# A two-layer decoder trunk on one core: turned attention product, and the seven-product form of the first half's first MLP from its first rows on

## The chip, the core and the metric

The kernel runs on one core of a Trainium2 chip. The metric is the device time of one execution in microseconds (us). Before the change it is 2275.01 us in the median of three runs (2270.06 to 2276.08).

## The reference, cut to what matters

The input is 1024 rows of width 1024 in float32, and two layers follow each other. Layer 0 mixes by sliding-window attention and, beside it, a gated DeltaNet of four heads; layer 1 mixes by a gated linear recurrence. After each mixer stands a layer norm, then an MLP with squared ReLU, then another layer norm.

```python
o = jnp.einsum('bnhgqk,bnkhd->bnqhgd', p.astype(v.dtype), vb)   # attention: softmax weights times values
...
def sqrelu_mlp(x, w1, w2):
    h = jax.nn.relu(x @ w1)
    return (h * h) @ w2
...
for layer in range(DEPTH):
    ...
    x = layer_norm(DN_ALPHA * x + mix, ln1_g[layer], ln1_b[layer])
    x = layer_norm(DN_ALPHA * x + sqrelu_mlp(x, mlp_w1[layer], mlp_w2[layer]), ln2_g[layer], ln2_b[layer])
```

There are 8 query heads of width 64 on 2 key heads, and a block of 128 rows sees its own 128 keys and those of the block before. The hidden width of the MLP is 4096.

## The kernel before, in words

**Two streams.** The rows are cut into two halves of 512, each a Python generator (`stream`): stream 0 for the first half, stream 1 for the second. Each goes through the layer-0 mixer (`hybrid`), its output projection and layer norm (`mix_out`), the first MLP (`mlp_ln`, `mlp`), the recurrence and its projection, and the second MLP. A planner at the end of `trunk` takes pieces from the streams and from a list of side jobs (`mixers`: attention blocks, DeltaNet heads, layer norms, the sums below) by a model of the engines' time, and so writes one fixed order for TensorE (PE); the order on the other engines follows from it. Nothing is reordered at run time.

**Large products.** A product in float32 is split into three in a rounded format (`mm3`, L206 holds every matmul): high times high, high times low, low times high, each with 128x128 weights and 512 columns moving, summed in a PSUM bank. Weights come by DMA into `ws` (three buffers, issued from the SP queue), are rounded into `wh` and the rest into `wl`, on ScalarE (ACT) or VectorE (DVE). The tiles `wh`, `wl` have three buffers too. PSUM has eight banks: four named `mm` for the large products, four named `mx` for the side jobs.

**The MLP.** It goes over four quarters `j` of the hidden width. In the straight form (`straight`) an eighth of the hidden rows is made with `w1` and at once multiplied with `w2`; a quarter takes 192 products with `w1` and 192 with `w2`. In the seven-product form (`first`, then `seven`) a quarter's hidden rows stay in two granules `g` of SBUF, and the product with `w2` is done as a 2x2 block product with seven block multiplications instead of eight, 168 products, with combinations of the hidden blocks on DVE (1024 elements wide) and four sums of `w2` blocks, `t1` to `t4`, that side job `w2_sums` makes in DRAM beforehand: a copy DRAM to DRAM from the SP queue and an adding copy from the POOL queue for each, 32 pairs in all, paced at 8 us a transfer in layer 0. In `seven` two results stay in PSUM over several block products: X in two `mm` banks, R in two `mx` banks, whose value is needed again with the third and fifth products. `weave` sets two pieces of `seven` beside one of `first` for the next quarter.

Which form is taken is decided at the loop `while e < 8`: the straight form goes on until stream 1 has its output projection in this layer, two granules are free and a quarter ends. Of the first half's first MLP the first two quarters are straight.

**Attention.** `attn_block` scores a block, exponentiates on ACT with the row sums in `den`, scales the weights by 1/`den` in 8 ACT instructions, turns them by transposes on PE (`csb` holds the identity), and multiplies: `vraw` (values, 64 wide) as weights, turned scores of 512 columns moving, plain float32, once for each key block and key head. The result is already turned for the output projection.

**Parked results.** In stream 1 ten projections for the DeltaNet (`park`, source `hin_fm`) are written to DRAM (`parked<-r`) and read back (`f<-parked`) when their head is due. `head_z` and `head_front` then work on them on ACT and DVE; tiles `f` have four buffers. `head_mid` of a head inverts a triangular matrix by steps of 32x32 matmuls (`mx<-t` 32x32), each with a few small DVE instructions between.

Of the kernel before, what the change touches and what calls it, by code (L numbers as in the profile page):

```python
# [17 lines left out]
P = 128  # L18
# [195 lines left out]
def trunk(ctx: ExitStack, tc, I, out):  # L214
# [316 lines left out]
    def mlp(layer, c, yT, yg, ls, res, tail=False):  # L531
# [65 lines left out]
        def seven(j, g, done):  # L597
# [8 lines left out]
            yield from wait(lambda: (layer, j) in summed)  # L606
            A = {f"a{r + 1}{q + 1}": v4(g[q])[:, :, r * 256:(r + 1) * 256] for q in range(2) for r in range(2)}
            bank = {}
            for i, (a, b, acc, out, sign, last) in enumerate((
# [4 lines left out]
                if i == 2:  # L614
                    V.tensor_tensor(A["a21"], A["a21"], A["a22"], ALU.subtract)
                elif i == 3:
                    V.tensor_tensor(A["a21"], A["a21"], A["a11"], ALU.subtract)
                elif i == 4:
                    V.tensor_tensor(A["a12"], A["a12"], A["a21"], ALU.add)
                elif i == 5:  # L620
                    V.scalar_tensor_tensor(A["a21"], A["a21"], -1.0, A["a22"], ALU.mult, ALU.subtract)
                start = i < 3
                if start:
                    bank[acc] = [(mm_ps if acc == "X" else mx_ps)() for _ in range(2)]
                    kept[0] += 2 * (acc == "X")
                for p in range(2):
                    yield from wait(lambda: either(2))
                    ring = either(2)
                    ah, al = ts(ring, F32R), ts(ring, F32R)
                    ah2, al2 = (z.rearrange("p (k t) -> p k t", k=2) for z in (ah, al))  # L630
                    x = A[a][:, 2 * p:2 * p + 2]
                    S.copy(ah2, x)
                    V.tensor_tensor(al2, x, ah2, ALU.subtract)
                    wh, wl = wblock(w2_quarter(layer, j, b)[p * P:(p + 1) * P])
                    for k in range(2):
                        for t in range(2):
                            mm3(bank[acc][t], ah2[:, k, t * P:(t + 1) * P], al2[:, k, t * P:(t + 1) * P], wh[k], wl[k],
                                start and p + k == 0, p + k == 2, not start)
                            if p + k == 2:
                                accumulate(bank[acc][t], 2 * out[0] + t, out[1], sign, done and last)  # L640
                            if k + t < 2:
                                yield
                    free(ring, ah, al)
                    if i == 6 and p == 1:
                        free("g", *g)
                        kept[0] -= 2
                    if done and i in (4, 6) and p == 1:
                        res["n"] = 2 + (i == 6) * 2
                    yield UNIT
# [67 lines left out]

        hids = {}
        e = 0
        while e < 8 and not ((c == 1 or sts[1].get("op", -1) >= layer) and rings["g"] >= 2 and e % 2 == 0):  # L720
            if e == 7:
                res["start"]()
            yield from straight(e, e == 7)
            e += 1
# [93 lines left out]
    def attn_block(c, n, st, oT, tl, o):  # L818
# [34 lines left out]
        S.activation(es, es, AF.Exp)  # L853
        V.tensor_tensor(den, den, es, ALU.add)
        V.reciprocal(den, den)
        for m in (0, 2, 1, 3):
            for g2 in range(2):
                i = 2 * (2 * (m // 2) + g2) + m % 2
                S.activation(pm[m][:, g2, :w], pm[m][:, g2, :w], AF.Copy, scale=den[:, i:i + 1])
        yield at(*pm)  # L860
        po = mx_ps()
        pend = None
        for i, (_, vv) in enumerate(keys):
            for h in range(2):
                ps = mx_ps()
                for g in range(4):
                    PE.transpose(ps[:, g * P:(g + 1) * P], pm[2 * (g // 2) + h][:, g % 2, i * P:(i + 1) * P], ident)
                pT = tl[(6, 7, 2, 3)[2 * i + h]]
                (S.copy if h else V.tensor_copy)(pT, ps)
                yield at(pT)  # L870
                PE.matmul(po[h * 64:(h + 1) * 64, :], vv[:, h * 64:(h + 1) * 64], pT, start=(i == 0),
                          stop=(i == len(keys) - 1))
        h, l = oT.quad(0, n)
        split_ps(h, l, v4(po))
        yield lambda: 0.0


# [501 lines left out]
    def stream(c):  # L1379
        s = dict(ln0=st[c])  # L1380
        xT, oT = xTs[c], ActT()
        yield from hybrid(c, xT, oT, st[c], ("t", "s") if c == 0 else ("t",))
        yield from mix_out(I["hout"], oT, lambda n: I["x"][c * CH + n * P:c * CH + (n + 1) * P, :], 0,
                           "s" if c == 0 else "t", s, st[c]["t"], lambda: c == 0 or "m7" in sts[0])
        phase[c] = 1
        if c == 0:
            spawn(w2_sums())
        yield from mlp_ln(0, c, s, "ts"[c], False)
        phase[c] = 0
        hT = ActT()  # L1390
# [163 lines left out]
```

## Time and profile before

| | |
|---|---|
| median of three runs | 2275.01 us |
| the profiled execution itself | 2275.25 us, of it 2273.5 us from the first to the last instruction |
| PE busy | 2212.7 us (97%) |
| DVE busy | 1546.0 us (68%) |
| ACT busy | 1048.4 us (46%) |
| mean granted TensorE clock | 0.993 |

In the profile, PEld are weight loads on TensorE, POOL is GpSimd, SP the queue that issues most transfers. A row of a group gives what was computed from what, its shape, its count, the busy time in us and the mean of one in ns, then the idle time ahead of it and what ended that. Shares of the clock of 1.00 are full speed. Almost every instruction of ACT and DVE carries L178 and every matmul L206, since helpers issue them; the tile names tell them apart. A plain float32 matmul shows as two instructions.

### The profile page before, as it was taken

How to read it: one execution, taken by the hardware profiler on the slowest of the kernel's cores; microseconds unless marked ns; L12 is line 12 of the kernel's file. 1: busy time of each engine (PE TensorE's matmuls, PEld its weight loads, DVE VectorE, ACT ScalarE, POOL GpSimd, SP SyncE). 2: the span in 40 equal slices, each digit the busy share in tenths (PEclk: the TensorE clock that was granted, in tenths of full speed). 3: DMA queues.
4: the chain of work that ended last, by engine and by line, in shares of the span. 5: the costliest groups of instructions: out<-in, count | busy, mean ns of one | idle time of the engine just before them, and what ended most of it. 6: DMA issues, size and time to landing. Idle time of an engine off the chain costs nothing.

```text
span 2273.5 us, 31954 instructions
## 1 busy us (share of the span) xinstructions
PE 2212.7 (97%) x12436; PEld 1788.5 (79%) x12436; DVE 1546.0 (68%) x2809; ACT 1048.4 (46%) x1878; POOL 28.6 (1%) x56
## 2 busy tenths in 40 slices
PE   8999999989999999999999999999999999999997
PEld 7776877758778887888887878878788887888886
DVE  6787676576555567596567898685566657776477
ACT  5365456244322344454444677373434444444442
POOL 0000000000000000000000000000000000000000
PEclk9999999989999999999999999999999999999999
DMA  4121223256667766677765333323533443444341
GB/s 162 57 77 49 94 79 112 84 181 181 188 199 221 210 209 201 205 251 224 237 214 184 126 134 115 127 83 98 179 103 123 140 145 128 150 169 146 122 164 67
DMA packets 89945, 337.46 MB, mean 148 GB/s; under 512 B 9921, under 2 KB 10305, under 8 KB 81601
## 3 DMA queue, kind: packets, MB, share of 16 engines
q1 hardware_dynamic: 76688, 280.56, 36.2%
q0 software_dynamic: 4608, 33.56, 7.8%
q10 hardware_dynamic: 8496, 21.30, 2.7%
q8 instruction: 97, 1.59, 0.3%
q14 instruction: 56, 0.45, 0.1%
HBM read 324.37 MB, written 78.12 MB: 177 GB/s over the span
## 4 chain that ended last, share of the span: by engine, by line
PE 85%; DVE 7%; ACT 5%; DMA 2%; issue 1%; ACTq 0%; SPq 0%; DVEq 0%
PE mm L206 67%; PE mx L206 17%; DVE g L178 2%; PE mx L210 2%; DVE wl L178 2%; ACT g L178 1%; DVE s L178 1%; ACT s L178 1%; ACT wh L178 1%; DVE t L178 1%; DVE f L178 1%; ACT t L178 1%; ACT f L178 1%; DMA f<-parked 1%; DMA parked<-r 0%
## 5 line engine op out<-in xcount | busy, mean ns | idle before, releaser
L206 PE MATMUL mm<-g,wh 128*128 128x512 f32 x2816 | 885.6, 396 | 1.1 <-DVE g L178 1.1
L178 DVE TENSOR_TENSOR wl<-ws,wh 128x1024 fp32r<-128x1024 f32 (+1 forms) x444 | 538.3, 1212 | 398.9 <-ACT wh L178 394.4
L178 ACT CAST wh<-ws 128x1024 fp32r<-128x1024 f32 (+1 forms) x356 | 371.3, 1043 | 663.4 <-PE mm L206 551.3
L206 PEld LDWEIGHTS mm<-g,wh 128*128 128x128 f32 x2816 | 521.5, 189 | 109.1 <-DVE g L178 2.8
L206 PE MATMUL mm<-g,wl 128*128 128x512 f32 x1408 | 550.3, 391 | 0.0
L206 PE MATMUL mm<-wh,s 128*128 128x512 f32 x1152 | 377.4, 394 | 0.7 <-DVE g L178 0.7
L206 PEld LDWEIGHTS mm<-g,wl 128*128 128x128 f32 x1408 | 265.4, 188 | 56.5
L206 PEld LDWEIGHTS mm<-wh,s 128*128 128x128 f32 x1152 | 216.9, 188 | 46.5 <-ACT s L178 1.1
L206 PE MATMUL mm<-wh,g 128*128 128x512 f32 (+1 forms) x768 | 240.0, 384 | 7.1 <-ACT wh L178 6.8
L206 PE MATMUL mm<-wl,s 128*128 128x512 f32 x576 | 224.8, 390 | 0.0
L206 PE MATMUL mx<-wh,s 128*128 128x512 f32 x576 | 187.9, 392 | 1.5 <-DVE s L178 1.5
L206 PEld LDWEIGHTS mm<-wh,g 128*128 128x128 f32 x768 | 143.3, 191 | 34.1 <-ACT wh L178 6.8
L178 ACT CAST s<-g 128x512 fp32r<-128x512 f32 x172 | 104.7, 622 | 103.2 <-PE mm L206 54.2
L178 DVE TENSOR_TENSOR s<-g,s 128x512 fp32r<-128x512 f32 x172 | 116.0, 685 | 44.3 <-ACT s L178 44.2
L206 PE MATMUL mm<-wl,g 128*128 128x512 f32 (+1 forms) x384 | 144.2, 375 | 0.2 <-DVE wl L178 0.2
L206 PEld LDWEIGHTS mx<-wh,s 128*128 128x128 f32 x576 | 108.2, 188 | 24.6 <-DVE s L178 2.4
L206 PEld LDWEIGHTS mm<-wl,s 128*128 128x128 f32 x576 | 108.6, 189 | 21.4 <-issue 0.2
L206 PE MATMUL mx<-wl,s 128*128 128x512 f32 x288 | 112.1, 389 | 0.0
L178 DVE CAST wh<-ws 128x1024 fp32r<-128x1024 f32 x88 | 60.4, 687 | 65.0 <-PE mm L206 57.7
L178 DVE TENSOR_TENSOR g<-g,mm 128x512 f32<-128x512 f32 x136 | 89.0, 682 | 11.9 <-PE mm L206 11.3
L178 ACT ACTIVATE g<-mm 128x512 f32<-128x512 f32 x100 | 59.2, 592 | 75.2 <-PE mm L206 75.2
L206 PEld LDWEIGHTS mm<-wl,g 128*128 128x128 f32 x384 | 73.5, 192 | 11.6 <-DVE wl L178 0.5
(234 smaller groups left out, 2390.7 us busy)
## 6 DMA issues: line engine op xcount, KB each, us to landing
ws<-w SPq DMA_DIRECT2D x232, 512.0 KB, 3.4
ws<-t SPq DMA_DIRECT2D x96, 512.0 KB, 3.4
t<-w POOLq DMA_DIRECT2D x32, 1024.0 KB, 9.1
ws<-hin_fm SPq DMA_DIRECT2D x32, 512.0 KB, 3.3
t<-w SPq DMA_DIRECT2D x16, 1024.0 KB, 6.8
t<-t SPq DMA_DIRECT2D x16, 1024.0 KB, 6.3
ws<-rin SPq DMA_DIRECT2D x32, 512.0 KB, 3.3
ws<-hout SPq DMA_DIRECT2D x16, 512.0 KB, 3.7
```

The source lines that it names most:

```text
L178: r = f(*a, **k)
L206: ins = self.pe.matmul(out, lhsT, rhs, start=start, stop=stop, skip_group_check=fresh)
L210: return self._pe(self.pe.transpose(out, x, ident), out, [x], 0.00042 * 2 * out.shape[-1])
```

## The change

It has four parts.

1. Attention: the exponentials are no longer scaled on ACT. The turned scores serve as weights (128x128) and the values move (64 columns), 16 matmuls a block (8 in the first), into one bank `po`, one after the other. One DVE instruction multiplies `po` by 1/`den` into `y`, four transposes on PE turn `y`, and the split into high and low part follows as before.
2. `seven` gets a form `brief` while stream 1 has not had its output projection in this layer: the third product is added to two outputs at once, and the fifth begins a fresh pair of `mx` banks, so R is held for one product only.
3. The choice of the form: the MLP of the first half in layer 0 waits for four free granules and then starts with `seven` at once; in layer 1 the straight form ends ahead of stream 1's projection only if all 14 granules are free.
4. `w2_sums` is spawned ahead of the first half's first output projection instead of behind it.

```diff
+            brief = sts[1].get("op", -1) < layer
...
-                    ("a21", "t1", "R", (1, 1), 1, False), ("a21", "t2", "X", (0, 1), -1, False),
+                    ("a21", "t1", "R", ((1, 1), (0, 1)) if brief else ((1, 1),), 1, False),
...
-                start = i < 3
+                start = i < 3 or brief and i == 4
...
-                                accumulate(bank[acc][t], 2 * out[0] + t, out[1], sign, done and last)
+                                for out in outs:
+                                    accumulate(bank[acc][t], 2 * out[0] + t, out[1], sign, done and last)
...
-        while e < 8 and not ((c == 1 or sts[1].get("op", -1) >= layer) and rings["g"] >= 2 and e % 2 == 0):
+        room = lambda: rings["g"] >= (2 if c == 1 or sts[1].get("op", -1) >= layer else
+                                      4 if layer == 0 else GB)
+        yield from wait(lambda: c == 1 or layer == 1 or room())
+        while e < 8 and not (room() and e % 2 == 0):
...
-        for m in (0, 2, 1, 3):
-            for g2 in range(2):
-                i = 2 * (2 * (m // 2) + g2) + m % 2
-                S.activation(pm[m][:, g2, :w], pm[m][:, g2, :w], AF.Copy, scale=den[:, i:i + 1])
...
-                PE.matmul(po[h * 64:(h + 1) * 64, :], vv[:, h * 64:(h + 1) * 64], pT, start=(i == 0),
-                          stop=(i == len(keys) - 1))
+                yield lambda: 0.0
+        yield at(*pT.values())
+        po = mx_ps()
+        for g in range(4):
+            for h in range(2):
+                o = po[:, (2 * g + h) * 64:(2 * g + h + 1) * 64]
+                for i, (_, vv) in enumerate(keys):
+                    PE.matmul(o, pT[i, h][:, g * P:(g + 1) * P], vv[:, h * 64:(h + 1) * 64], start=(i == 0),
+                              stop=(i == len(keys) - 1))
+        y = tl[3]
+        V.tensor_tensor(y.rearrange("p (i d) -> p i d", i=8), po.rearrange("p (i d) -> p i d", i=8), bc_last(den, 64),
+                        ALU.mult)
+        yield at(y)
+        ps = mx_ps()
+        for g in range(4):
+            PE.transpose(ps[:, g * P:(g + 1) * P], y[:, g * P:(g + 1) * P], ident)
...
+        if c == 0:
+            spawn(w2_sums())
         yield from mix_out(I["hout"], oT, lambda n: I["x"][c * CH + n * P:c * CH + (n + 1) * P, :], 0,
...
-        if c == 0:
-            spawn(w2_sums())
```

Over the whole program, the orders of before and after differ in these counts on PE: products of 512 columns 48 fewer (two quarters in the seven-product form, 24 fewer each); 30 matmuls `64x512` of attention gone, 120 of `128x64` in their place (60 and 240 instructions); 32 more transposes. On DVE 44 instructions more, on ACT 44 fewer.

The order on PE around the first half's first layer norm, before. `mm` rows with `wh_5187` are the first products of its first MLP, `csb` rows from `g_4290` and `g_4291` the transposes of the normed rows, `mx<-t` 32x32 the inversion in a head of the second half.

```order
L206 MATMUL mm_5024<-g_2008,wl_5021 128x512
L206 MATMUL mx_5077<-t_4413 32x32 x16
L210 MATMUL mx_5096<-csb,g_4290 128x128 x4
L210 MATMUL mx_5124<-csb,g_4291 128x128 x4
L210 MATMUL mx_5134<-csb,g_4291 128x128 x4
L206 MATMUL mx_5144<-t_4413 32x32 x16
L210 MATMUL mx_5162<-csb,g_4291 128x128 x4
L210 MATMUL mx_5169<-csb,g_4291 128x128 x4
L206 MATMUL mm_5191<-g_4818,wh_5187 128x512
L206 MATMUL mm_5191<-g_4819,wh_5187 128x512
```

The same place after, where `g_4160` and `g_4161` are the normed rows and `mm_4926` is a parked projection of the second half:

```order
L206 MATMUL mm_4926<-g_2041,wl_4923 128x512
L210 MATMUL mx_4942<-csb,g_4160 128x128 x4
L210 MATMUL mx_4952<-csb,g_4160 128x128 x4
L206 MATMUL mm_4926<-g_2041,wh_4922 128x512
L206 MATMUL mm_4926<-g_2042,wh_4922 128x512
L206 MATMUL mm_4926<-g_2041,wl_4923 128x512
L210 MATMUL mx_4962<-csb,g_4160 128x128 x4
L210 MATMUL mx_4990<-csb,g_4161 128x128 x4
L206 MATMUL mm_4926<-g_2041,wh_4922 128x512
L206 MATMUL mm_4926<-g_2042,wh_4922 128x512
L206 MATMUL mm_4926<-g_2041,wl_4923 128x512
```

Before, 96 products of parked projections stand between the output projection and the first product of the MLP, and five of the eight groups of transposes stand behind the last of them. After, 168 stand there: 72 that stood ahead of the output projection (216 there before, 144 now) have moved behind it. They lie among the transposes, and 60 large products stand between the last of the transposes and the MLP.

The order on PE inside an attention block, before, `mm_4628` being a projection that lies beside it:

```order
L206 MATMUL mm_4628<-wh_4671,g_1136 128x512
L206 MATMUL mx_4687<-g_147,vraw_3099 64x512
L210 MATMUL mx_4704<-csb,g_146 128x128 x2
L210 MATMUL mx_4704<-csb,g_147 128x128 x2
L206 MATMUL mm_4629<-wh_4671,g_1135 128x512
L206 MATMUL mm_4629<-wl_4672,g_1135 128x512
L206 MATMUL mm_4629<-wh_4671,g_1136 128x512
L206 MATMUL mm_4626<-wh_4715,g_1371 128x512
```

And after, from the last transposes of a block (`mx_3972`) to its first products with the values:

```order
L210 MATMUL mx_3972<-csb,g_146 128x128 x2
L210 MATMUL mx_3972<-csb,g_147 128x128 x2
L206 MATMUL mx_3978<-t_3404 32x32 x16
L206 MATMUL mm_3925<-g_2039,wh_3921 128x512
L206 MATMUL mm_3925<-g_2040,wh_3921 128x512
L206 MATMUL mm_3925<-g_2039,wl_3922 128x512
L206 MATMUL mm_3925<-g_2041,wh_3921 128x512
L206 MATMUL mm_3925<-g_2042,wh_3921 128x512
L206 MATMUL mm_3925<-g_2041,wl_3922 128x512
L206 MATMUL mx_4003<-vraw_3045,g_147 128x64
L206 MATMUL mx_4003<-vraw_3050,g_147 128x64
L206 MATMUL mx_4003<-vraw_3045,g_146 128x64
```

The four groups of transposes that took turns with the matmuls now stand together, and the 16 products of 64 columns follow in one run.

The order on DVE where the parked results are read back, before. `f_5071` is the last gate read back; `f_5642`, `f_5653`, `f_5664` are the reads of the last head; `t_4413` is the inversion of the head before it.

```order
L178 SCALAR_TENSOR_TENSOR f_5070<-f_5070,f_5071 128x512
L178 TENSOR_TENSOR t_4413<-t_4413,mx_5195 128x128
L178 STREAM_TRANSPOSE t_4413<-t_4413 128x128
L178 TENSOR_TENSOR g_4833<-f_5070,g_4832 128x512
L178 SCALAR_TENSOR_TENSOR f_5643<-f_5642,sm,f_5643 128x512 x3
L178 TENSOR_TENSOR t_4413<-mx_5224,csb 128x128
L178 SCALAR_TENSOR_TENSOR f_5654<-f_5653,sm,f_5654 128x512 x3
L178 TENSOR_TENSOR t_4413<-t_4413,mx_5251 128x128
L178 CAST wh_5420<-ws_5418 128x1024
L178 STREAM_TRANSPOSE t_4413<-t_4413 128x128
L178 SCALAR_TENSOR_TENSOR f_5665<-f_5664,sm,f_5665 128x512
```

And after, with `f_5242` as the last gate, `f_5733` and `f_5744` as reads of the last head and `t_4652` as the inversion:

```order
L178 SCALAR_TENSOR_TENSOR f_5241<-f_5241,f_5242 128x512
L178 CAST wh_5493<-ws_5491 128x1024
L178 TENSOR_TENSOR wl_5494<-ws_5491,wh_5493 128x1024
L178 TENSOR_TENSOR g_4812<-f_5241,g_4811 128x512
L178 TENSOR_TENSOR t_4652<-t_4652,mx_5349 128x128
L178 STREAM_TRANSPOSE t_4652<-t_4652 128x128
L178 SCALAR_TENSOR_TENSOR f_5734<-f_5733,sm,f_5734 128x512 x2
L178 TENSOR_TENSOR t_4652<-mx_5377,csb 128x128
L178 SCALAR_TENSOR_TENSOR f_5734<-f_5733,sm,f_5734 128x512
L178 SCALAR_TENSOR_TENSOR f_5745<-f_5744,sm,f_5745 128x512
L178 TENSOR_TENSOR t_4652<-t_4652,mx_5404 128x128
```

In both, small steps of the inversion stand behind instructions that need what was read back; after the change there are two weight instructions (`wh_5493`, `wl_5494`) among them, and the steps lie closer.

More of the change, by code (lines that the diff above doesn't have):

```diff
@@ L608, in seven @@
             bank = {}
-            for i, (a, b, acc, out, sign, last) in enumerate((
[4 rows of a table removed]
+            brief = sts[1].get("op", -1) < layer
+            for i, (a, b, acc, outs, sign, last) in enumerate((
+                    ("a12", "b21", "R", ((0, 0),), 1, False), ("a11", "b11", "X", ((0, 0),), 1, True),
+                    ("a21", "t1", "R", ((1, 1), (0, 1)) if brief else ((1, 1),), 1, False),
+                    ("a21", "t2", "X", ((0, 1),), -1, False),
+                    ("a12", "b22", "R", ((0, 1),), 1, True), ("a21", "t3", "X", ((1, 1),), -1, True),
+                    ("a22", "t4", "X", ((1, 0),), 1, True))):
                 if i == 2:
@@ L855, in attn_block @@
         V.reciprocal(den, den)
-        for m in (0, 2, 1, 3):
-            for g2 in range(2):
-                i = 2 * (2 * (m // 2) + g2) + m % 2
-                S.activation(pm[m][:, g2, :w], pm[m][:, g2, :w], AF.Copy, scale=den[:, i:i + 1])
[L860 to L864, printed above, removed]
+        pT = {}
+        for h in range(2):
+            yield at(pm[h], pm[2 + h])
+            for i in range(len(keys)):
                 ps = mx_ps()
@@ L867, in attn_block @@
                     PE.transpose(ps[:, g * P:(g + 1) * P], pm[2 * (g // 2) + h][:, g % 2, i * P:(i + 1) * P], ident)
-                pT = tl[(6, 7, 2, 3)[2 * i + h]]
-                (S.copy if h else V.tensor_copy)(pT, ps)
-                yield at(pT)
-                PE.matmul(po[h * 64:(h + 1) * 64, :], vv[:, h * 64:(h + 1) * 64], pT, start=(i == 0),
-                          stop=(i == len(keys) - 1))
+                pT[i, h] = tl[(6, 7, 2, 4)[2 * h + i]]
+                (S.copy if i else V.tensor_copy)(pT[i, h], ps)
+                yield lambda: 0.0
+        yield at(*pT.values())
+        po = mx_ps()
+        for g in range(4):
+            for h in range(2):
+                o = po[:, (2 * g + h) * 64:(2 * g + h + 1) * 64]
[9 more added lines that the diff above has]
+            PE.transpose(ps[:, g * P:(g + 1) * P], y[:, g * P:(g + 1) * P], ident)
         h, l = oT.quad(0, n)
-        split_ps(h, l, v4(po))
+        split_ps(h, l, v4(ps))
         yield lambda: 0.0
```

3 rows, old and new, of the table bank are left out of this document.

## The prediction

> **What bounds the kernel now.** I read the page first, then the table of windows in pieces of 100 us, then the waits, the chain and the timeline where the windows showed a gap.
>
> The first row of the page: busy time of each engine, its share of the span, its instructions.
>
> ```profile
> PE 2212.7 (97%) x12436; PEld 1788.5 (79%) x12436; DVE 1546.0 (68%) x2809; ACT 1048.4 (46%) x1878; POOL 28.6 (1%) x56
> ```
>
> PE is busy in all but 61 us of 2273.5. So two kinds of gain exist: fewer columns on PE, and those idle 61 us. The windows around the places that the change touches (span of the window, then busy us of PE, PEld, DVE, ACT, POOL, granted clock, busy share of the DMA engines, GB/s):
>
> ```profile
> 400.00:500.00 100.00, 88.73 (x652) 65.92 (x651) 70.79 (x168) 39.72 (x77) 1.04 (x2) 0.95 0.40 129
> 500.00:600.00 100.00, 100.00 (x770) 78.63 (x769) 54.18 (x122) 37.65 (x82) 4.20 (x6) 0.96 0.63 175
> 600.00:700.00 100.00, 100.00 (x762) 80.83 (x761) 55.59 (x127) 38.20 (x91) 4.45 (x6) 1.00 0.70 201
> 1000.00:1100.00 100.00, 100.00 (x443) 82.84 (x442) 68.96 (x88) 47.56 (x64) 2.46 (x3) 1.00 0.75 228
> ...
> 470.00:480.00 10.00, 5.49 (x54) 4.04 (x54) 9.86 (x18) 5.44 (x10) 0.00 (x0) 0.69 0.97 360
> 469.60:508.50 38.90, 27.63 (x312) 19.77 (x302) 25.02 (x45) 14.30 (x26) 1.04 (x2) 0.78 0.65 209
> ```
>
> From 500 us on PE is full while the two straight quarters run; at 1000 us it is full with the seven-product form. The gap of 400 to 500 us lies whole between 469.6 and 508.5: PE is idle there for 38.90 - 27.63 = 11.3 us, at a mean clock of 0.78. What PE waited for between 460 and 510 us (total, times, longest), and the chain there (start, length):
>
> ```profile
> PE mx L206 <- DVE t L178: 8.2, 5, 4.7
> PE mx L210 <- DVE g L178: 3.1, 1, 3.1
> ```
>
> ```profile
> 439.87 8.17 PE mm L206 x36
> ...
> 449.63 2.17 DMA parked<-r
> 451.81 3.06 DMA f<-parked
> ...
> 470.67 7.59 DMA parked<-r
> 478.34 3.77 DMA f<-parked
> 487.25 7.31 DMA f<-parked
> 498.88 4.14 PE mm L206 x9
> 503.82 4.14 PE mm L206 x9
> 508.48 2.27 PE mm L206 x9
> ```
>
> Two things come together. The transposes of the layer norm (the 3.1 us on DVE `g`) have no large products left to lie among: the parked projections are used up and the MLP needs the norm. And ACT and DVE stand still for the last parked results, with steps of a head's inversion queued behind them, for which PE waits in order:
>
> ```profile
> 494.67 0.72 ACT L178 ACTIVATE f<-f,sm 128x512 f32<-128x512 f32 x1 [7.26 <-DMA f<-parked]
> 495.43 0.75 DVE L178 SCALAR_TENSOR_TENSOR f<-f,sm,f 128x512 f32<-128x512 f32 x1 [4.78 <-ACT f L178]
> ```
>
> After the longest wait nine products take 4.14 us, twice, and then 2.27: 3.7 us more, and some 0.4 on the small matmuls among them. That place costs 11.3 + 4.1 = 15.4 us.
>
> **The sevens.** A full stretch gives the price of a large product:
>
> ```profile
> 709.58 96.02 PE mm L206 x423
> ```
>
> That is 0.227 us each. Two quarters lose 24 products each: 48 x 0.227 = **10.9 us off PE**, in a stretch where PE is full, so it comes off the end. What it adds lies beside PE:
>
> ```profile
> L178 DVE TENSOR_TENSOR wl<-ws,wh 128x1024 fp32r<-128x1024 f32 x436 | 532.6, 1222 | 398.5 <-ACT wh L178 394.4
> L178 DVE TENSOR_TENSOR s<-g,s 128x512 fp32r<-128x512 f32 x172 | 116.0, 685 | 44.3 <-ACT s L178 44.2
> L178 DVE TENSOR_TENSOR g<-g,g 128x1024 f32<-128x1024 f32 x24 | 29.3, 1219 | 0.0
> ```
>
> For a quarter, 14 weight blocks instead of 8 and 14 hidden pieces instead of 8 and four combinations: 6 x 1.22 + 6 x 0.685 + 4 x 1.22 = 16.3 us of DVE. The accumulations are 16 either way, since the brief form adds its third product twice. A quarter takes (192 + 168) x 0.227 = 82 us, so DVE goes from 55% to some 75%, near the 69% at which PE was full at 1000 us. I cost it at nothing; without that cover it would be at most 2 x 16 us. Holding R for one product only leaves the four `mx` banks to the side jobs in between, so the heads of the second half do not wait for a seven to end. The wait for four free granules stops only stream 0; the order shows stream 1's parked projections filling the time.
>
> **Attention.** Rows of the old form: a large product, the product with the values (two instructions), four transposes, a large product. Then a single load of 128 weights and four of them in a row (whose matmuls move only 16 columns); then four instructions with 128 columns moving, and the lengths of all such (shortest, median, longest, in ns).
>
> ```profile
> 424.78 0.40 PE L206 MATMUL mm<-wh,g 128*128 128x512 f32 x1
> 425.11 1.07 PE L206 MATMUL mx<-g,vraw 128*64 128x512 f32 x2
> 426.11 0.66 PE L210 MATMUL mx<-csb,g 128*128 128x128 f32 x4
> 426.52 0.48 PE L206 MATMUL mm<-wh,g 128*128 128x512 f32 x1
> ```
>
> ```profile
> 122.91 0.19 PEld L206 LDWEIGHTS mm<-g,wl 128*128 128x128 f32 x1
> ...
> 273.13 0.52 PEld L206 LDWEIGHTS mx<-dsc,csb 128*128 128x128 f32 x4 [0.52 <-DVE dsc L178]
> ```
>
> ```profile
> 123.37 0.60 PE L206 MATMUL mx<-S,t 128*128 128x128 f32 x4
> ```
>
> ```profile
> L206 PE MATMUL mx<-S,t x88: 270/275/377, 114.7 to 694.5; 128*128 128x128 f32 x88
> ```
>
> ```profile
> L206 PE MATMUL mx<-g,vraw 128*64 128x512 f32 x60 | 32.2, 618 | 0.0
> ```
>
> The large product would have made room at 424.78 + 0.227 = 425.01; the next thing began at 426.11. So an old product with values costs 1.10 us, 30 of them 33.0. The new form has 240 instructions, each with a load of 128 weights and 64 columns. It is not in the trace. One load after another in the row of four takes (0.52 - 0.19)/3 = 0.11 us. The stream of 512 columns took 1.07 - 0.62 = 0.45 (618 ns is one of the two, 1.07 both), so 64 columns an eighth of it, 0.056. Lower bound 0.056 each (loads free), upper 0.11 + 0.056 = 0.166 (nothing overlaps). I take 0.11, from the row with the same weights and still fewer columns: 26.4 us, and 8 x 0.2 for entering and leaving. Four more transposes a block at 426.52 - 426.11 = 0.41 are 3.3. Together 31.3 against 33.0: **1.7 us off**, between 14.7 off and 11.7 on.
>
> Here the Trainium skill speaks against the change: its page "TensorE: Matmul & The Clock Gate", Part 3, under what overlaps and what doesn't, says that a weight load overlaps a running matmul only when the row group differs. By that rule all 240 loads would stand in the open and attention would cost 11.7 us more instead. The row of four with 128 columns, all in one row group, does not bear it out here: the four together take 0.60 us, a single one 0.275, so they follow at 0.11, where load and stream one after the other would need 0.22.
>
> The scalings that leave ACT (8 a block) and the DVE instruction that comes (8 x some 0.69, as every one of 512 elements) are off PE's path, but they shorten a block by the time between the sums and the transposes:
>
> ```profile
> 417.76 3.31 ACT L178 ACTIVATE g<-g,asc 128x256 f32<-128x256 f32 x8 [0.18 <-DVE asc L178]
> ```
>
> 3.3 us a block that PE does not wait for, yet the first half's mixer is through earlier: that is why the planner sets its output projection ahead of 72 more parked products. New waits are the matmuls with values for the last copy, and the last transposes for the DVE instruction. Behind the first PE has two triples and an inversion step, 1.8 us, against a copy of 0.7; I cost it at nothing, at most 8 x 0.5.
>
> **The gap at 470 us.** 72 products x 0.227 = 16.3 us of cover move behind the output projection, where the norm's transposes now lie among them. The 3.1 us on the norm go. The parked results stay: the last of them is copied when PE leaves the last parked product. In the quick round above the write was issued 1.6 us after that (448.04 to 449.63), write and read took 5.2, and from a read's landing (482.11) to the end of its DVE work
>
> ```profile
> 484.24 0.69 DVE L178 TENSOR_TENSOR g<-f,g 128x512 fp32r<-128x512 f32 x1
> ```
>
> ```profile
> 469.22 0.45 PE L206 MATMUL mx<-t 32*32 32x32 f32 x32
> ```
>
> are 2.8 (to 484.93): 9.6 us in all. The last row is an inversion step on PE. In the slow round, 7.59 and 3.77 for write and read, it is 15.8. In the new order PE has 36 large products and three inversion steps of some 0.4 until it needs DVE behind that, 9.4 us. The wait is 0.2 to 6.4 us, I take the middle, 3.3. The last head's third read (7.31 above, 4.78 of wait on DVE) now has a weight instruction (1.22) and an inversion step or two more ahead of it on DVE, some 1.7 us, so up to 3.1 remains; 1.7. That leaves 5.0 of the 15.4, **10.4 us off**; the ends are 0.2 and, with another half-clock stretch of 4.1, 13.6.
>
> **The sums** go past the loads for the first output projection on SP. The mean DMA share there is 0.40 (400 to 500 us), and three `ws` buffers are cover, so I cost it at nothing; without them a load behind a sum is late by no more than the 7.31 us above; on POOL nothing is queued behind them that PE needs.
>
> **The sum.** Against the profiled execution's own 2275.25 us (span 2273.5 and 1.75 around it; the median is 0.24 lower): 2275.25 - 10.9 - 1.7 - 10.4 = **2252**. Its own range is 2243 to 2261, by the ends of the gap.
>
> **Rivals.** *The gap stays* (16%): the parked round trips now run beside the sums, which begin earlier, and the whole 15.4 us comes back elsewhere. For it: the one read beside a sum took 7.31 us. Against it: four transfers of 512 KB that shared the 0.97 window have gone from that place. Time 2275.25 - 12.6 = 2263.
>
> *The loads show* (9%): 240 x 0.056 = 13.4 us more, 2266. For it: no row has this shape. Against it: the row of four loads and the row of four matmuls. The rule of the Trainium skill quoted there would give the same.
>
> *Weights come late* (7%), the slower side: a round of `weave` is 24 + 24 products, 10.9 us, and needs three blocks of 512 KB, one in 3.6 us, where the straight form needed one in 5.4. The sums of layer 0 run beside it. The DMA share would lie between the 0.75 of 1000 us, where the sums go more slowly, and half more than the 0.63 to 0.70, all of it. At 0.97 a transfer of 256 KB took 7.59 us; a block would then take some 15, and the buffers cover 10.9 less 2.3 for rounding, 8.6. Each round would be 6.6 us late, and seven of the 14 rounds 46: 2298. It turns the sign from the fifth late round on. Against it: at 1000 us the same form ran full at 0.75 beside sums.
>
> *Nothing gained* (7%): the gap stays and the loads show, 2275.
>
> **How the numbers follow.** About 0.3% of this kernel, 6.8 us, can be told from no change. The forecast has 61%. Faster: 61 + 16 + 9 = 86%; same 7%; slower 7%. The range of 2241 to 2267 takes in the forecast, the first two rivals and some of the cheaper loads; outside are the last two, and some 6% below.
>
> **What would show it.** Right: 240 rows of `mx<-vraw,g` at about 26 us of PE; PE without the 3.1 us wait on `g` and with at most some 5 us on `t` before the MLP; PE full, at clock 1.00, through the first two quarters; 48 large products fewer. Wrong: waits on `wh` or `wl` in those quarters, matmul instructions 0.17 us apart in the attention, or a clock under 0.9 at the start of the MLP.

## The result, and the profile after

The changed kernel takes **2282.26 us** (median of nine, 2277.92 to 2285.74) where the kernel before takes 2270.95: a ratio of 1.0055 [1.0045, 1.0065], 0.55% slower. The prediction was 2252, with 2241 to 2267 as its range. One of the nine runs of before, at 2574 us, is left out of the ratio; the others lie between 2267.16 and 2276.08, with a median of 2270.5.

A caution for the reading: the profiled execution of after is the lowest of its nine (2277.92), and that of before, 2275.25, is one of its higher ones. The two pages differ by less than the kernels do, so a second trace of before, at 2266.31 us, stands beside them below.

The first row of the page after: busy time of each engine, share of the span (2276.1), instructions.

```profile
PE 2202.8 (97%) x12600; PEld 1806.5 (79%) x12600; DVE 1580.9 (69%) x2853; ACT 1039.4 (46%) x1834; POOL 29.4 (1%) x56
```

PE is busy 9.9 us less than before, and yet the span is 2.6 us longer: PE's idle time went from 60.8 to 73.3 us. The saving was made, and came back as waits. The windows of after (span, busy us of PE, PEld, DVE, ACT, POOL, granted clock, DMA share, GB/s) show where:

```profile
340.00:360.00 20.00, 15.21 (x222) 12.72 (x220) 10.42 (x26) 8.05 (x24) 0.82 (x1) 0.91 0.64 167
460.00:510.00 50.00, 39.13 (x436) 30.03 (x435) 27.46 (x53) 16.89 (x31) 1.66 (x2) 0.93 0.65 193
500.00:600.00 100.00, 95.56 (x772) 75.02 (x772) 65.61 (x136) 43.94 (x95) 4.31 (x7) 0.98 0.70 200
600.00:700.00 100.00, 96.70 (x741) 76.88 (x740) 66.87 (x135) 43.23 (x92) 4.07 (x5) 0.98 0.70 206
```

The same two early windows in the second trace of before:

```profile
340.00:360.00 20.00, 19.28 (x140) 15.36 (x139) 12.83 (x40) 11.93 (x36) 0.00 (x0) 1.00 0.54 179
460.00:510.00 50.00, 42.64 (x449) 31.95 (x436) 38.13 (x68) 24.99 (x43) 1.85 (x3) 0.93 0.68 213
```

So PE loses time in three places. At 340 to 360 us PE now loses 4.8 us instead of 0.7. At 460 to 510 it loses 10.9; the profiled execution of the prediction had 11.3 there, but the second trace only 50 - 42.64 = 7.4. And the two new quarters, where PE was full, lose 4.4 and 3.3 us, with the clock below 1.00. What PE waits for in after, in three stretches (300 to 400 us, 460 to 510, 500 to 700; total, times, longest):

```profile
PE mx L210 <- DVE g L178: 5.6, 2, 4.5
...
PE mx L206 <- DVE t L178: 10.9, 4, 6.2
...
PE mx L206 <- DVE t L178: 4.8, 4, 3.0
PE mx L210 <- DVE t L178: 2.8, 1, 2.8
```

PE has no wait on `wh` or `wl` among these, and the weight loads (PEld) wait 0.4 us for each of the two between 500 and 700 us, so the weights of the new quarters come in time. PE waits for `t` and `g`, steps of the heads of the second half that lie on DVE. The same view of before's second trace at 460 to 510:

```profile
PE mx L206 <- DVE t L178: 4.3, 4, 1.7
PE mx L210 <- DVE g L178: 3.0, 1, 3.0
```

The norm's wait on `g` is gone in after, as was forecast; the wait on `t` is more than double that of this trace (and 10.9 for the 8.2 of the profiled execution). Some lines of the chain of after name what is behind it:

```profile
343.50 9.50 DMA parked<-r
353.05 2.67 DMA f<-parked
...
475.69 6.78 DMA parked<-r
482.86 8.69 DMA parked<-r
491.56 2.86 DMA f<-parked
499.73 3.93 PE mm L206 x9
504.05 2.27 PE mm L206 x9
```

These are parked round trips, writes of 256 KB among them, and behind the last of them nine products that take 3.93 us where the next nine take 2.27. The first piece of a DRAM sum on SP's queue, in after and then in the profiled execution of before:

```profile
313.46 0.61 SPq L178 DMA_DIRECT2D t<-w  x1
```

```profile
479.32 0.60 SPq L178 DMA_DIRECT2D t<-w  x1
```

The sums now start 166 us earlier and lie beside every parked round trip. The median of a parked write in 300 to 510 us (last column, us to landing) rose from before to after:

```profile
parked<-r SPq DMA_DIRECT2D x10, 256.0 KB, 2.0
```

```profile
parked<-r SPq DMA_DIRECT2D x10, 256.0 KB, 4.8
```

In the new quarters the cause is another one. The DVE queue of after around the wait that PE has at 671 us (start, length, operation), and PE's own rows there:

```profile
667.40 1.22 DVE L178 TENSOR_TENSOR g<-g 128x1024 f32<-128x1024 f32 x1
668.54 1.22 DVE L178 TENSOR_TENSOR wl<-ws,wh 128x1024 fp32r<-128x1024 f32 x1
669.67 1.22 DVE L178 TENSOR_TENSOR g<-g,g 128x1024 f32<-128x1024 f32 x1
670.81 0.68 DVE L178 TENSOR_TENSOR g<-g,mx 128x512 f32<-128x512 f32 x1
671.41 0.28 DVE L178 TENSOR_TENSOR t<-t,mx 128x128 f32<-128x128 f32 x1
671.60 0.68 DVE L178 TENSOR_TENSOR g<-g,mx 128x512 f32<-128x512 f32 x1
672.20 0.68 DVE L178 TENSOR_TENSOR s<-g,s 128x512 fp32r<-128x512 f32 x1
672.80 1.22 DVE L178 TENSOR_TENSOR wl<-ws,wh 128x1024 fp32r<-128x1024 f32 x1
673.94 0.30 DVE L178 STREAM_TRANSPOSE t<-t 128x128 f32<-128x128 f32 x1
```

```profile
671.04 0.39 PE L206 MATMUL mm<-g,wl 128*128 128x512 f32 x1
674.39 0.65 PE L206 MATMUL mx<-t 32*32 32x32 f32 x32 [2.96 <-DVE t L178]
674.97 1.22 PE L206 MATMUL mm<-g,wh 128*128 128x512 f32 x2
```

DVE works without a break from 667.40 to 674.24. Two of its pieces, `g<-g` and `g<-g,g` of 1024 elements, are combinations of the seven products. Behind them, the stream transpose that an inversion's next matmuls need is done only at 674.24; PE, which takes its work in order, stands 2.96 us for it, and the two products behind take 1.22 us where a pair took 0.62 or 0.63 just before.

### The profile page after: what moved, and what is told of

It reads as the page before. It is cut to its first block, busy times and chain, and to the rows that moved or that the text cites. A ratio compares the mean times of both kernels' runs of the same rounds, so it can differ in the third digit from the quotient of the medians.

```text
span 2276.1 us, 32349 instructions
## 1 busy us (share of the span) xinstructions
PE 2202.8 (97%) x12600; PEld 1806.5 (79%) x12600; DVE 1580.9 (69%) x2853; ACT 1039.4 (46%) x1834; POOL 29.4 (1%) x56
## 4 chain that ended last, share of the span: by engine, by line
PE 85%; DVE 9%; ACT 3%; DMA 2%; issue 1%; ACTq 0%; DVEq 0%; SPq 0%
PE mm L206 65%; PE mx L206 18%; DVE g L178 4%; DVE wl L178 2%; PE mx L210 2%; DMA parked<-r 1%; DVE t L178 1%; DVE s L178 1%; ACT wh L178 1%; DMA f<-parked 0%; ACT t L178 0%; ACT g L178 0%; DVE f L178 0%; ACT s L178 0%; ACT f L178 0%
## 5 line engine op out<-in xcount | busy, mean ns | idle before, releaser
L178 DVE TENSOR_TENSOR wl<-ws,wh 128x1024 fp32r<-128x1024 f32 (+1 forms) x456 | 552.9, 1213 | 359.6 <-ACT wh L178 354.5
L206 PE MATMUL mm<-wh,s 128*128 128x512 f32 x960 | 312.1, 392 | 1.2 <-ACT r L178 0.7
L206 PE MATMUL mx<-wh,s 128*128 128x512 f32 x672 | 221.8, 394 | 1.7 <-DVE s L178 1.7
L206 PEld LDWEIGHTS mm<-wh,s 128*128 128x128 f32 x960 | 180.2, 188 | 40.0 <-ACT r L178 1.2
L206 PE MATMUL mm<-wl,s 128*128 128x512 f32 x480 | 186.9, 389 | 0.0
L178 ACT CAST s<-g 128x512 fp32r<-128x512 f32 x200 | 121.5, 623 | 129.8 <-PE mm L206 61.6
L178 DVE TENSOR_TENSOR s<-g,s 128x512 fp32r<-128x512 f32 x200 | 134.8, 686 | 48.6 <-ACT s L178 48.3
L206 PEld LDWEIGHTS mx<-wh,s 128*128 128x128 f32 x672 | 126.2, 188 | 28.9 <-DVE s L178 3.0
L206 PE MATMUL mx<-wl,s 128*128 128x512 f32 x336 | 131.1, 390 | 1.1 <-DVE wl L178 1.1
L206 PEld LDWEIGHTS mm<-wl,s 128*128 128x128 f32 x480 | 90.2, 188 | 18.3 <-issue 0.2
L206 PEld LDWEIGHTS mm<-wl,g 128*128 128x128 f32 x384 | 73.3, 191 | 11.4 <-DVE wl L178 0.6
```

The source lines that it names most:

```text
L178: r = f(*a, **k)
L206: ins = self.pe.matmul(out, lhsT, rhs, start=start, stop=stop, skip_group_check=fresh)
```

## The experiments

The theories as the expectations name them. **A**: the sums that begin earlier run beside the parked round trips, and PE waits for these. **B**: the new order by itself puts inversion steps and transposes where PE must wait. **C**: the seven-product quarters are not supplied in time beside the sums. After the first four kernels C took a definite form, **D**: an inversion step's DVE work queues behind combinations and pieces of the seven products. Each ratio is to the kernel before on the same chip, whose median was 2269.01, 2269.05, 2268.18, 2267.87 and 2270.71 us in the five groups of runs.

**The attention alone**: before with the attention's part of the diff.

> The attention part alone, on the kernel before (2271 us by the median of nine runs). Its order on PE puts the first output projection 72 products earlier, as the whole change does, but the MLP stays straight and the sums start where they did. Theory A (the whole change is slower because the sums in DRAM, begun earlier, run beside the parked round trips): attention by itself gains on PE and in the gap before the first MLP, 2260 to 2267. Theory B (the new order itself puts inversion steps and transposes where PE waits for them, with or without the sums): 2275 or more.

2279.17 us, 1.0043 [1.0029, 1.0058]: some 10 us slower, where 1.7 faster was forecast. The table of instructions shows why half of it isn't the attention's: this kernel has 24 large products more than before (rows of `mm<-wh,t` 128 for 64, of `mx<-wh,s` 528 for 576, and half as many of `wl` with each). Its order of events made the old rule for free granules leave one more quarter of stream 0's first MLP straight. So a later kernel holds it to four straight eighths, as before has:

```diff
         while e < 8 and not ((c == 1 or sts[1].get("op", -1) >= layer) and rings["g"] >= 2 and e % 2 == 0):
+            if c == 0 and layer == 0 and e == 4:
+                yield from wait(lambda: sts[1].get("op", -1) >= layer and rings["g"] >= 2)
+                break
```

> The kernel before with the new attention, as measured alone before (2279.2 us), but made to hold to four straight eighths in stream 0's first MLP, as the kernel before has them; with the attention alone the rule for free granules let six run straight, 24 large products of 0.227 us more. Theory: 5.4 of those ten us are these products, so 2271 to 2275 us. Rival: the attention's own order costs the ten, and they stay, 2277 to 2281 us. The forecast's 1.7 us gain would be 2267.

2273.08 us, 1.0015 [1.0003, 1.0027]. The extra quarter cost 5.3 us (4.9 above before instead of 10.2), as 24 x 0.227 = 5.4 says. Some 5 us of the attention's order remain without the sevens. B would have it so, but this run doesn't show B: with the mixer through earlier, the first sum of this kernel starts at 453.75 us (479.32 before), and both of PE's waits between 460 and 600 us, 5.4 and 3.7, end a chain that comes from a parked transfer, a write of 8.09 us at 460.67 and a read of 8.02 at 508.72. So A has a part in them.

**The sums at their old place**, the changed kernel otherwise:

```diff
-        if c == 0:
-            spawn(w2_sums())
         yield from mix_out(I["hout"], oT, ...
         phase[c] = 1
+        if c == 0:
+            spawn(w2_sums())
```

> The whole change, with the sums spawned behind the first output projection as before; the order on PE is the same as the changed kernel's, row for row. Theory A: the waits on parked results shrink, 2250 to 2262, 20 us or more below the changed kernel. Theory B: within 4 us of the changed kernel, 2278 to 2286. Theory C (the seven-product quarters ask for more weight loads than the DMA engines give beside the sums): also 2278 to 2286, since those quarters still run beside the sums.

2270.94 us, 1.0008 [0.9995, 1.0022]: 9.4 us below the changed kernel, each against its own before (+1.9 and +11.3). The early sums cost that much, but A alone doesn't bring the forecast back. The same edit the other way, before with nothing but the early sums:

> The kernel before with one line moved: the sums spawned ahead of the first output projection. The order on PE is the same as the kernel's before. Theory A: 8 to 20 us slower than before, 2279 to 2291, with waits of ACT on parked results of 30 us or more against 14.9. Theories B and C: within 4 us of before, 2267 to 2275.

2277.83 us, 1.0035 [1.0025, 1.0045]: 8.8 us slower, with before's order on PE, a little under what A expected. Transfers of its chain, the read of 11.03 us longer than any of before's:

```profile
464.40 5.43 DMA parked<-r
469.88 11.03 DMA f<-parked
483.83 6.61 DMA f<-parked
493.76 4.99 DMA f<-parked
```

PE loses 16.4 us at 460 to 510 here, where the two traces of before have 11.3 and 7.4. That is A in the time and on the chain; the sign that was expected with it, waits of ACT on parked results of 30 us or more, did not come (16.1 us at 300 to 700, for 14.9 before). **No sums at all**, the changed kernel reading plain blocks in their place:

```diff
-        return tsum[layer][j][q] if q in SUMS else I[f"w2_{layer}"][j * 4 + QUARTER[q]]
+        q = dict(t1="b11", t2="b22", t3="b12", t4="b21").get(q, q)
+        return I[f"w2_{layer}"][j * 4 + QUARTER[q]]
```

> The whole change without the sums in DRAM (no copies, no adding copies; the seven-product form reads plain blocks of w2 in their place, so the output is another one); same order on PE. Theory A: 2248 to 2258, and no wait of ACT on a parked result over 4 us. Theory B: 2278 to 2286. Theory C: like A; apart from A only by the run with late sums.

2263.71 us, 0.9972 [0.9961, 0.9983]. Another 7.2 us go (from +1.9 to -5.3), so sums at the old place cost too; with the new order they start at 455.83 us there, beside the round trips, not at 479.32. Yet the forecast isn't reached, and the two new quarters still lose the same time without any sums. These windows of this kernel are nearly those of after, at a DMA share of 0.27 and 0.34:

```profile
500.00:600.00 100.00, 95.56 (x726) 76.21 (x725) 63.73 (x131) 44.92 (x94) 0.10 (x1) 0.97 0.27 89
600.00:700.00 100.00, 96.69 (x732) 77.16 (x731) 67.81 (x138) 42.24 (x92) 0.00 (x0) 0.98 0.34 112
```

That rules the sums out as the cause of the idle time there, and led to D. **The sevens alone** (old attention, old place of the sums):

> The kernel before with the seven-product quarters alone: old attention, sums begun at the old place. With the new attention this is 2270.9 us. Theory D: the quarters save 10.9 us and lose about as much in the two waits, so 2266 to 2273 us, and the waits are there. Rival T (the new attention and the order that it brings cost some 5 us, also where no quarter turns straight for it): 2261 to 2266 us. Rival U (the sevens themselves cost more than they save, and the attention brings the 1.7 us that was forecast): 2272 to 2276 us.

2272.36 us, 1.0010 [1.0000, 1.0021]. 48 products fewer, and 3.3 us slower: 14.2 us are lost to something that came with the quarters. PE waits 5.5 us on `t` between 500 and 700 us here; the wait that ends at 578 us stands behind a combination and a weight piece on DVE, the one that ends at 553 behind a weight piece and small steps, without a combination. With the attention on top (the kernel with late sums) it is 1.4 us less, so the attention, with the gap that it was to shorten, brings 1.4 in this order. The other order gives another split: the attention alone with four straight eighths is at +4.9, and the sevens on top of it bring 3.0.

**Without the combinations** in stream 0's first MLP, sums late (the planner is told of them, so that PE's order stays):

```diff
-                if i == 2:
+                if c == 0 and layer == 0:
+                    if 2 <= i <= 5:
+                        o, q = (("a21", "a22"), ("a21", "a11"), ("a12", "a21"), ("a21", "a22"))[i - 2]
+                        c0, c1 = clk.NS["V"]
+                        clk.issue("V", [A[o]], [A[o], A[q]], c0 + c1 * 1024)
+                elif i == 2:
```

> The changed kernel with the sums begun at the old place, and without the four combinations of activations that each seven-product quarter of stream 0's first MLP makes on DVE (they are left out, so the output is another one; the order on PE is that of the kernel with the late sums, 2270.9 us). Theory D (the two new quarters give back what they save: an inversion step's DVE work queues behind combinations and pieces, and PE, in order, stands some 3 us for it twice, with slow products behind): the two waits fall below 1.5 us each, 2259 to 2266 us. Rival S (PE's order or the weights make those waits, not the combinations): both waits stay, 2268 to 2273 us.

2258.97 us, 0.9951 [0.9935, 0.9967]: 12.0 us below the kernel with them (-10.1 against +1.9). The two new quarters run nearly full again:

```profile
500.00:600.00 100.00, 98.99 (x768) 78.55 (x767) 63.54 (x134) 46.27 (x100) 4.30 (x7) 1.00 0.71 202
600.00:700.00 100.00, 99.93 (x758) 80.43 (x758) 67.41 (x140) 46.37 (x101) 4.29 (x5) 1.00 0.78 227
```

DVE is as busy as in after (63.54 and 67.41 against 65.61 and 66.87), and PE hardly waits. D holds, and the busy share of DVE has little to do with it. Not all of the 12.0 belongs to the new quarters: the edit leaves the combinations out in all four quarters of this MLP, and at 800 to 900 us, where the two older ones have them, PE's idle time is 1.2 us instead of 3.3. **The same combinations in halves**, each made right ahead of the pieces that read it, eight of 0.69 us in place of four of 1.22 a quarter:

```diff
-                elif i == 3:
-                    V.tensor_tensor(A["a21"], A["a21"], A["a11"], ALU.subtract)
...
+                halves = c == 0 and layer == 0
+                if not halves:
+                    mix(0, 4)
...
                 for p in range(2):
                     yield from wait(lambda: either(2))
+                    if halves:
+                        mix(2 * p, 2 * p + 2)
```

> The changed kernel with the sums begun at the old place (2270.9 us), each combination of stream 0's first MLP made in two halves of 512 elements, each right ahead of the pieces that need it (8 x 0.69 us on DVE for 4 x 1.22; the order on PE is the same). Theory D: DVE's bursts get shorter, the two waits of 3 us fall to 1 to 2.5, 2263 to 2269 us. Rival S: no change, 2269 to 2273 us.

2265.40 us, 0.9982 [0.9971, 0.9993]: 5.6 us less than in one piece, though DVE has more to do. On the changed kernel itself, sums early:

> The changed kernel as it is, sums begun early, with the combinations of stream 0's first MLP in halves as the only edit (the order on PE is the same). If the combinations and the early sums cost independently of each other: 2282.3 - 5.5, so 2275 to 2279 us. If the early sums cost because they make the weights of the two new quarters late, and the halves then have nothing to gain: 2280 to 2284 us.

2273.97 us, 1.0015 [1.0005, 1.0026]: 8 us less than the changed kernel (+3.3 against +11.3), a little more than expected. The early sums don't hide the combinations.

**Both costs away**: no sums, and no combinations there.

> The changed kernel without the sums in DRAM (plain blocks of the second weights are read instead) and without the combinations on DVE in stream 0's first MLP: both are left out, so the output is another one; the order on PE is the changed kernel's. Theory D plus A (two costs in two places, each about 7 to 12 us): without the sums it was 2263.7 us, without the combinations the kernel with late sums went 12 us down, so both together 2250 to 2254 us. Rival (the costs hide behind each other, or the gap at 470 to 505 us grows into what is saved): 2256 to 2262 us.

2249.51 us, 0.9904 [0.9889, 0.9920], from four runs. That is 21.2 us below before, where the forecast, 2252 against 2275.25, was 23.2 below. It is no kernel to use, since its output is another one, and it also lacks the combinations and sums that before has. At the place of the gap PE loses 3.0 us:

```profile
460.00:510.00 50.00, 46.97 (x477) 35.63 (x476) 28.55 (x51) 18.61 (x34) 0.10 (x1) 0.97 0.36 122
```

**Sums moved out of the round trips' way.** Two ways were tried, on the kernel with late sums and halves (2265.40). One makes the sums of the first two quarters from the first projections on, and all others once the first seven has begun:

```diff
         for layer, j in ((i, j) for i in range(2) for j in range(4)):
+            yield from wait(lambda: (layer, j) < (0, 2) or begun)
...
+        if c == 0:
+            spawn(w2_sums())
         spawn(delta_scalars(c, st))
```

> The kernel with late sums and halved combinations (2265.4 us), its sums for the first two quarters of layer 0 made already from the first projections on, before any parked projection is written, and all others only once the first seven-product quarter has begun, after the last parked result is read. The order on PE is nearly the same. Theory A (sums cost by making the parked round trips slow, for which PE waits at 345 to 360 and 470 to 505 us): the waits there fall, 2257 to 2263 us. Rival B (the sums' traffic costs the same wherever it lies, since the loads of weights are then late): 2264 to 2270 us.

2268.47 us, 1.0000 [0.9991, 1.0010]: slower by 3.9 than with late sums (+0.3 against -3.6), not faster. At 460 to 510 us PE gains (44.65 busy for 40.05), but at 100 to 200 it loses more; the kernel with late sums and halves, and then this one:

```profile
100.00:200.00 100.00, 94.82 (x660) 78.48 (x659) 80.74 (x236) 56.61 (x175) 0.61 (x6) 0.98 0.20 63
```

```profile
100.00:200.00 100.00, 87.00 (x631) 73.87 (x630) 75.26 (x235) 54.51 (x171) 3.90 (x10) 0.95 0.48 131
```

One wait of 7.5 us on DVE `t` stands there; its chain has a load of 7.20 us for the second half's input (`ws<-xT`). So in this kernel a sum costs beside a load that a chain of small steps waits for; A was too narrow. The same kernel with casts moved from DVE to ACT in that MLP:

```diff
-        (V.tensor_copy if wcount[0] % HV == 0 else S.copy)(h, x)
+        (V.tensor_copy if wcount[0] % HV == 0 and not (begun and phase[0] == 1 and phase[1] == 0) else S.copy)(h, x)
```

> As the kernel with the sums of two quarters in front, and while stream 0 alone is in its first MLP every cast of a weight block goes to ACT, where one in five goes to DVE (0.69 us each) otherwise. Theory D (what is left of the two new quarters' waits is DVE's queue ahead of an inversion step): 1 to 4 us below the same kernel with the casts on DVE. Rival: no difference above 1 us, or slower, since ACT's queue also holds copies of inversion steps.

2268.54 us, 0.9997 [0.9985, 1.0009]: no difference, though DVE has no cast left at 500 to 700 us where it had seven. What is left of those quarters' waits isn't the casts. The other way lets the first quarter's sums go between the two groups of round trips, at 5 us a transfer instead of 8:

```diff
+            yield from wait(lambda: len(reads) >= 2 and (layer + j == 0 or begun))
```

> The kernel with late sums and halved combinations (2265.4 us), its sums for the first quarter alone made between the two groups of parked round trips (they are let go after the second parked read and land mostly before the second group is read back), all other sums only once the first seven-product quarter has begun. The order on PE is the same. Theory A (beside parked round trips sums cost most, since PE waits for these): the waits at 470 to 505 us fall and none comes elsewhere, 2257 to 2262 us. Rival B (they cost wherever PE runs on loads without a stretch of large products, so the waits only move): 2263 to 2268 us.

2264.70 us, 0.9983 [0.9974, 0.9992]: within the spread of the halves alone, so no gain that can be told. The last copy of that quarter's sums was issued at 447.90 us and its adding copy at 454.06, among the writes of the second group, and the median of these writes (430 to 510 us) is 6.2 us where it is 2.1 with late sums. Of the kernels that leave nothing out, this one and the halves beat before, by 0.17 and 0.18%.

**Before once more**, for its second trace:

> The kernel before once more, for a second trace of it: the profiled execution that the prediction started from took 2275.25 us, the median of 31 is 2269. If the 15.4 us lost at 470 to 508 us are what this kernel usually loses there, a trace at about 2269 us shows PE idle for some 11 us in that place and the difference lies elsewhere. If that execution was an unlucky one, a trace at about 2269 us shows 5 to 8 us there.

2266.31 us. PE loses 7.4 us at 460 to 510 instead of 11.3, and its wait on `t` is 4.3 instead of 8.2, at a clock of 0.93 instead of 0.83. The execution on which the prediction worked, at 2275.25 us, was an unlucky one at just that place; this one, below the median of 2269, is rather a lucky one.

## Why the prediction was wrong

The forecast was 23.2 us down, the result 11.3 up: 34.5 us apart. The experiments split it into three steps that failed: 14.2 in the sevens, 10.7 in the gap, 9.4 in the sums, together 34.3. The parts add up because each is what the forecast gave a step less what one run after another measured for it. With the attention ahead of the sevens the same runs give 7.9 for the sevens and 17.0 for the attention with the gap, so of these two only the sum, 24.9, is firm.

**The sevens: the 10.9 us off PE were right, "I cost it at nothing" was wrong.** Rows of large products in before, and then in after:

```profile
L206 PE MATMUL mm<-wh,s 128*128 128x512 f32 x1152 | 377.4, 394 | 0.7 <-DVE g L178 0.7
L206 PE MATMUL mx<-wh,s 128*128 128x512 f32 x576 | 187.9, 392 | 1.5 <-DVE s L178 1.5
L206 PE MATMUL mm<-wh,t 128*128 128x512 f32 x64 | 20.4, 392 | 1.9 <-DVE g L178 1.8
```

```profile
L206 PE MATMUL mm<-wh,s 128*128 128x512 f32 x960 | 312.1, 392 | 1.2 <-ACT r L178 0.7 <-ACT s L178 0.5
L206 PE MATMUL mx<-wh,s 128*128 128x512 f32 x672 | 221.8, 394 | 1.7 <-DVE s L178 1.7
L206 PE MATMUL mm<-wh,t 128*128 128x512 f32 x128 | 40.2, 390 | 0.0
L206 PE MATMUL mx<-vraw,g 128*128 128x64 f32 x240 | 27.8, 273 | 0.0
```

The `wh` rows lose 192 - 96 - 64 = 32, and with half as many of `wl` that is the 48. The cover was judged by a share: DVE at 75% would be near the 69% at which PE was full at 1000 us. DVE came to 66 and 67%, lower still, and PE waited. The row at 1000 us could have told: it has 443 PE instructions in 100 us, and 443 x 0.227 = 100.6, so there were large products alone, and no chain of small steps through DVE. In the first quarters the heads of the second half invert alongside, PE is in order, and what counts is how much stands ahead of one 0.3 us step in DVE's queue. Taking the four combinations a quarter away gave 12.0 us back, on the kernel with the attention and in four quarters, not two; that most of what the sevens lost lay there is shown, how much exactly is not. The prediction's bound without cover, "at most 2 x 16 us", held the size; it was not put into the range.

**The attention: right on PE.** All 240 products came at 27.8 us busy, and a row of 32 of them on the timeline of after gives 3.68 / 32 = 0.115 us each, where 0.11 was taken:

```profile
394.26 3.68 PE L206 MATMUL mx<-vraw,g 128*128 128x64 f32 x32
```

So *the loads show* is out: one load and one stream in turn would be 0.166 us by the prediction's estimate, 39.8 in all. The Trainium skill ("TensorE: Matmul & The Clock Gate", Part 3, what overlaps and what doesn't) says that a weight load overlaps a running matmul only when the row group differs; this row, with all loads in one row group, contradicts it.

**The gap: 10.4 us forecast; with the attention's 1.7 that is 12.1, and 1.4 was measured.** The norm's wait went, as forecast. The rest failed twice. First, the 15.4 us were read off one execution: the second trace loses 3.9 us less of idle time there at a clock 0.10 higher. Second, "that leaves 5.0" priced the round trips by rows of before, where the first sum was issued only at 479.32 us. With the mixer through earlier, the sums start earlier too, at 455.83 us even from the old place in the code. Without any sums PE is idle for 3.5 us at that place at a clock of 0.93, and for 3.0 at 0.97 without the combinations too (above), so the round trips by themselves cost about the 5.0 that were to be left.

**The sums past the loads: "I cost it at nothing" cost 9.4 us** (8.8 on the kernel before). The argument was the mean DMA share of 0.40 and the three `ws` buffers. These cover weight loads, and the weights came in time. They don't cover a round trip with a chain behind it: write, read, ACT, DVE, an inversion step, PE. A write of 256 KB took 9.50 us at 343 us, in a window that the prediction gives no price, since PE lost only 0.7 us there before.

**The rivals.** *The gap stays* named this mechanism, beside the sums, at 16%, but its price ended at the gain it took back; a transfer that slows can cost more than an earlier gain. The rival on the slower side, *weights come late*, had the sign and the wrong mechanism: PE's loads waited 0.4 us each for `wh` and `wl` there. The range left out the uncovered ends of both steps that were costed at nothing. Two of the prediction's sums are also off, without bearing on the miss: by the ends of the gap its own range would begin at 2247 (2275.25 - 10.9 - 1.7 - 15.2), not 2243, and *nothing gained* adds up to 2276.

**Open**: how much of the 4.9 us of the attention's order, in a kernel without the sevens, is A and how much B; why both costs together give 4 us more than their sum (21.2 against 5.3 + 12.0); and whether sums that end before the second group's first write would gain, since the kernel made for it did not get them out of the way in time.

## What to carry to other kernels

An engine's busy share says whether work is supplied, not how long a small step waits in its queue: where an in-order engine waits for a chain of small steps through another, count what stands ahead of such a step, and cut long pieces into parts made right before they are read. A background transfer is free only beside a stretch of work that waits for nothing small, so look at every round trip that it will newly lie beside, also where nothing waits today. And price a wait from more than one execution: the same place lost 7.4 us in one trace and 11.3 in another of the same kernel.

## What the runs showed of the hardware

A DRAM write of 256 KB that landed in 2.0 us (median) took up to 9.50 beside a sum of 1 MB from DRAM to DRAM, and a read up to 11.03. After PE had stood 2.96 us at 671, the next pair of large products took 1.22 us instead of 0.63; with the sevens alone it took 1.22 after a wait of 2.37 us at 553, but 0.73 after one of 2.36 at 578, so the length of the wait alone doesn't decide it. Matmuls with 128 weights and 64 columns, each with its own load, follow each other at 0.115 us, about the 0.11 of a load alone: load and stream overlap. Executions of one kernel in one group of runs lay as far apart as 2265.19 and 2280.11 us.
